# A hybrid attention layer on one core: where weight tiles are split into high and low halves, and when

## The chip, the cores and the metric

The kernel runs on one core of a Trainium2 chip. The metric is the device time of one launch in microseconds (us). The engines are TensorE (PE in the profile), VectorE (DVE), ScalarE (ACT), GpSimd (POOL) and SyncE (SP), whose queue starts most loads.

## The reference, cut to what matters

One layer, for 2048 tokens of width 1024 in float32. A normalised input is projected by one wide matrix; its columns feed three groups of heads, whose gated outputs are joined, multiplied by `w_out`, added to `x` and normalised again:

```python
def hybrid_layer(x, norm_g, w_in, ..., w_out):
    z = jnp.einsum('bsd,de->bse', rmsnorm(x, norm_g), w_in)
    (aq, ak, av, ag, mq, mk, mv, mo, mi, mf, mg, gq, gk, gv, ga, gg) = jnp.split(z, split_idx, axis=-1)
    y_a = band_chunk_attention(aq, ak, av, rel_bias) * jax.nn.silu(ag)      # 6 heads, band of 9 chunks of 64
    h_ml = mlstm_chunkwise(q, k, mv, mi, mf)                                # 6 heads, after a causal convolution
    y_b = jax.nn.sigmoid(mo) * head_rmsnorm(h_ml, ml_norm_g, 6) * jax.nn.silu(mg)
    y_c = head_rmsnorm(gla_chunkwise(gq, gk, gv, log_alpha), gla_norm_g, 4) * jax.nn.silu(gg)
    y = jnp.concatenate([y_a, y_b, y_c], axis=-1)
    return x + jnp.einsum('bse,ed->bsd', y, w_out)
# and at the end: rmsnorm(x, final_g)
```

In the gated linear attention (GLA) the part inside a chunk carries a decay for each pair of tokens and each key channel:

```python
    decay = jnp.where(causal, jnp.exp(jnp.minimum(bcum[:, :, None] - bcum[:, None, :], 0.0)), 0.0)
    att = jnp.einsum('bthd,bjhd,btjhd->bhtj', qx, kx, decay)
```

## The kernel before

**Split operands.** Every float32 operand of the large matmuls is held in two halves: a high half, which is a cast on ACT (line 231 for weights), and a low half, the tile minus its high half, by a subtraction (line 232). Three matmuls for each piece of the contraction take high by high, high by low and low by high (lines 240 to 242 and 260 to 262; 1199 to 1201 and 1209 to 1211 in the output projection). The function `other()` gives the engine of a subtraction: every third call gives GpSimd, the others VectorE. Weight tiles live in a ring of five (`wring`), and their raw loads in three buffers (`wraws`).

**First phase.** The tokens are taken in four blocks of 512. For each block the projections run on PE one weight tile after the other. Between pieces of a projection a small scheduler (`Flow`) lets "chains" advance: gates, mLSTM, GLA and the preparation of the next block. One chain is `gla_in`, the GLA diagonal. In each block, for two halves of 256 tokens, GpSimd does 16 steps of two multiplications: `gk` (line 790) is the key times the decay so far and `prd` (line 793) its product with the query. After every four steps PE reduces four `prd` tiles into the bank `pw` (line 799), and the next steps overwrite them. `flow.chains` holds the names of the chains that are active at that point of the program.

**Second phase.** Attention runs by blocks of tokens, too. For a head and 128 tokens PE makes scores (`s`, line 1068); DVE adds the bias and finds the maximum (`pt`, `sm`, line 1084), ACT takes the exponential (1087), DVE the reciprocal (1088) and POOL scales (`pt`, 1089). PE transposes `pt` into `tp` (1128); ACT casts it to `ph` (1134) and DVE subtracts to `pl` (1135), and PE multiplies both with the values (1144, 1147). After a head, `w` is copied to `cc` by ACT (1161) and DVE (1162); after two heads POOL multiplies with the gate `gt` (1164), and `cc` is split into the tile `y` (1105, 1106). The attention of the first block (`attention0`) runs beside the last kept projections, beside `load_wo`, and beside the first ten parts of the output projection `out_mm` for block 0. After that each block's attention is merged with `out_mm` of the block before it.

**load_wo.** The eight row tiles of `w_out` are loaded in the order k = 3 to 7, then 0, 1, 2. The first five go into the weight ring. The last three are split in halves of 512 columns into `xs` tiles, so that they appear as `x`: three loads, six casts (line 1035) and six subtractions (line 1036). `put` holds each split back by three and then calls `split_late`, which fixes its place in the program order. The output projection of block 0 uses k = 3 to 7 in its first parts, and these `x` tiles after them.

**Order.** PE's order is the order of the code. On the other engines a list scheduler places the instructions, except where `keep_in_program_order` or `issue_after` binds them. `merge(a, b, na, nb, acc)` alternates steps of two generators; a negative `acc` lets `a` go ahead first. `load_final` loads the two halves of `final_g`, after the attention's latest key load. The final addition of `x` is in `out_mm` (loads at line 1191, addition at 1214).

## Time and profile before

| what | value |
|---|---|
| median of three runs | 1271.97 us (1270.75 to 1275.88) |
| the profiled execution | 1273.61 us |
| its span, first to last instruction | 1271.7 us |
| mean granted TensorE clock | 0.989 |
| first phase, about | 0 to 925 us |

A page of the profile gives the busy time of each engine, then the span in 40 slices of 31.8 us with a digit for the busy tenths of each; PEclk is the granted clock of TensorE in tenths. A row of a timeline is: start, length, engine, line, operation, output <- inputs with sizes, count, and in brackets the idle time of the engine before it and what released it. A row of waits is: engine, tile and line of the waiting instruction, what it waited for; total us, times, longest. A row of windows gives for each engine the busy us and the number of instructions (x), then the granted clock, the DMA engines' share and GB/s.

### The profile page before, as it was taken

What the parts mean: (1) busy time and instruction counts of PE and PEld (TensorE: products, weight loads), DVE (VectorE), ACT (ScalarE), POOL (GpSimd) and SP (SyncE); (2) the same over time, 40 slices, a digit from 0 to 9 for tenths busy, and PEclk for the clock granted to TensorE, in tenths of its full rate; (3) what the DMA queues carried; (4) which work ended last, traced back from release to release, by engine and by line L of the source; (5) the groups of instructions that cost most, each with busy time, mean ns of one, the idle gap of its engine ahead of it and who ended that gap; (6) DMA issues with size and microseconds to landing.
All of it is one profiled execution on the core that took longest, in us unless ns stands there. A gap on an engine that the chain in (4) does not pass through costs nothing.

```text
span 1271.7 us, 19323 instructions
## 1 busy us (share of the span) xinstructions
PE 1243.1 (98%) x6804; PEld 1009.3 (79%) x6804; DVE 813.6 (64%) x1869; ACT 590.2 (46%) x1097; POOL 594.4 (47%) x762
## 2 busy tenths in 40 slices
PE   8999999999999999999999999999979999999997
PEld 7777877788787778878777877787867878878886
DVE  6647746772775677376487876664577676766641
ACT  5636422553543355253324643332566566655631
POOL 3337652244856233385523555641464454454442
PEclk8999999999999999999999999999989999999999
DMA  6158344434623443372353242427796456455122
GB/s 247 34 149 278 96 143 138 128 101 128 251 84 126 126 132 98 106 276 73 110 150 118 75 129 86 141 68 221 239 274 193 151 187 209 159 194 164 50 86 81
DMA packets 100185, 184.31 MB, mean 145 GB/s; under 512 B 10592, under 2 KB 46304, under 8 KB 100088
## 3 DMA queue, kind: packets, MB, share of 16 engines
q1 hardware_dynamic: 95624, 174.94, 43.8%
q10 hardware_dynamic: 4464, 8.13, 1.7%
q8 instruction: 54, 0.88, 0.3%
q14 instruction: 43, 0.35, 0.1%
HBM read 147.34 MB, written 35.70 MB: 144 GB/s over the span
## 4 chain that ended last, share of the span: by engine, by line
PE 89%; DVE 3%; POOL 3%; DMA 2%; issue 1%; ACT 1%; SPq 1%; POOLq 0%; DVEq 0%; ACTq 0%
PE ip L240 14%; PE ip L241 13%; PE ip L242 13%; PE ip L260 4%; PE ip L261 4%; PE ip L262 4%; PE ip L1209 4%; PE ip L1211 4%; PE ip L1210 4%; PE s L1068 4%; PE tp L1128 3%; PE ga L851 2%; PE w L1147 2%; PE s L705 2%; PE w L1144 2%
## 5 line engine op out<-in xcount | busy, mean ns | idle before, releaser
L240 PE MATMUL ip<-x,w 128*128 128x512 f32 x784 | 319.0, 407 | 0.2 <-ACT vg L519 0.2
L241 PE MATMUL ip<-x,w 128*128 128x512 f32 x784 | 306.8, 391 | 0.0
L242 PE MATMUL ip<-x,w 128*128 128x512 f32 x784 | 306.6, 391 | 0.0
L240 PEld LDWEIGHTS ip<-x,w 128*128 128x128 f32 x784 | 147.7, 188 | 43.7 <-issue 13.6
L242 PEld LDWEIGHTS ip<-x,w 128*128 128x128 f32 x784 | 147.7, 188 | 32.3
L241 PEld LDWEIGHTS ip<-x,w 128*128 128x128 f32 x784 | 147.8, 189 | 28.0 <-issue 1.4
L231 ACT CAST w<-wraw 128x1024 fp32r<-128x1024 f32 x126 | 131.7, 1047 | 37.2 <-PE ip L262 9.8
L232 POOL TENSOR_TENSOR w<-wraw,w 128x1024 fp32r<-128x1024 f32 x42 | 101.8, 2424 | 98.2 <-ACT w L231 98.2
L232 DVE TENSOR_TENSOR w<-wraw,w 128x1024 fp32r<-128x1024 f32 x84 | 114.7, 1367 | 41.7 <-ACT w L231 41.3
L1089 POOL TENSOR_SCALAR pt<-pt,sm 128x640 f32<-128x640 f32 (+2 forms) x96 | 72.5, 759 | 119.4 <-DVE sm L1088 91.7
L793 POOL TENSOR_TENSOR prd<-gk,zg 128x16 f32<-128x16 f32 (+7 forms) x112 | 65.7, 586 | 78.1 <-PE pw L799 72.2
L260 PE MATMUL ip<-w,x 128*128 128x512 f32 x256 | 102.0, 398 | 0.0
L261 PE MATMUL ip<-w,x 128*128 128x512 f32 x256 | 99.8, 390 | 0.2 <-POOL w L232 0.2
L262 PE MATMUL ip<-w,x 128*128 128x512 f32 x256 | 99.7, 390 | 0.0
L1087 ACT ACTIVATE pt<-pt,sm 128x640 f32<-128x640 f32 (+2 forms) x96 | 73.2, 763 | 47.4 <-DVE sm L1084 43.6
L1135 DVE TENSOR_TENSOR pl<-tp,ph 128x512 fp32r<-128x512 f32 (+1 forms) x108 | 71.9, 673 | 36.1 <-ACT ph L1134 35.9
L1068 PE MATMUL s<-kk,qq 128*128 128x256 f32 (+2 forms) x360 | 81.9, 313 | 2.3 <-DVE sm L1084 2.2
L790 POOL TENSOR_TENSOR gk<-gk,al 128x16 f32<-128x16 f32 (+14 forms) x120 | 70.7, 590 | 22.0 <-ACT al L767 14.6
L1134 ACT CAST ph<-tp 128x512 fp32r<-128x512 f32 (+1 forms) x108 | 60.3, 572 | 41.3 <-PE tp L1128 39.0
L490 ACT ACTIVATE e<-ip 128x512 f32<-128x512 f32 x44 | 26.2, 595 | 106.6 <-PE ip L242 102.5
L1068 PEld LDWEIGHTS s<-kk,qq 128*128 128x128 f32 x360 | 62.5, 189 | 16.3 <-DVE sm L1084 5.8
L1128 PE MATMUL tp<-ident,pt 128*128 128x128 f32 x420 | 62.5, 274 | 2.5 <-POOL pt L1089 2.5
(352 smaller groups left out, 2491.2 us busy)
## 6 DMA issues: line engine op xcount, KB each, us to landing
wraw<-in_w_f SPq DMA_DIRECT2D x100, 512.0 KB, 3.7
wraw<-in_w_t SPq DMA_DIRECT2D x28, 512.0 KB, 3.6
qq<-q_d SPq DMA_DIRECT2D x48, 256.0 KB, 4.6
kk<-k_d SPq DMA_DIRECT2D x18, 512.0 KB, 5.9
vv<-v_d SPq DMA_DIRECT2D x18, 512.0 KB, 6.2
xraw<-in_xT SPq DMA_DIRECT2D x16, 512.0 KB, 8.5
xr<-in_x SPq DMA_DIRECT2D x16, 512.0 KB, 3.7
out<-xr ACTq DMA_DIRECT2D x31, 256.0 KB, 2.3
```

The source lines that it names most:

```text
L231: nc.scalar.copy(w[:, :, 0, :], rv)
L232: other().tensor_tensor(w[:, :, 1, :], rv, f32(w[:, :, 0, :]), op=ALU.subtract)
L240: nc.tensor.matmul(ps, w[:, k, 0, :], X[k][:, 0, :], start=(k == 0), stop=False)
L241: nc.tensor.matmul(ps, w[:, k, 0, :], X[k][:, 1, :], start=False, stop=False)
L242: nc.tensor.matmul(ps, w[:, k, 1, :], X[k][:, 0, :], start=False, stop=(k == KT - 1))
L260: nc.tensor.matmul(ps, X[k][:, 0, t], w[:, 0, :], start=(k == 0), stop=False)
L261: nc.tensor.matmul(ps, X[k][:, 0, t], w[:, 1, :], start=False, stop=False)
L262: nc.tensor.matmul(ps, X[k][:, 1, t], w[:, 0, :], start=False, stop=(k == KT - 1))
L1068: nc.tensor.matmul(sp[:, :cn], qq[:, l, tt * P:(tt + 1) * P], kk[:, ko + c0:ko + c0 + cn], start=(l == 0), stop=(l == 1))
L1087: nc.scalar.activation(pt[:, :n], pt[:, :n], AF.Exp, bias=init, scale=-1.0, accum_out=sm[:, 2:3])
L1089: nc.gpsimd.tensor_scalar(pt[:, :n], pt[:, :n], sm[:, 3:4], 0.5, op0=ALU.mult, op1=ALU.mult)
L1128: nc.tensor.transpose(out=tp[:, w + x_ * P:w + (x_ + 1) * P], in_=pt[:, (b - b0) * P:(b - b0 + 1) * P], identity=ident)
```

## The change

Four edits. First, `other()` gives GpSimd no work while the chain `gla_in` is active: its count goes on, and the first call after the diagonal goes to GpSimd. Second, the six half tiles of the last three `w_out` rows are no longer split among the heads of the first block. They are kept in a list, and after the first attention and `load_wo` have been issued, they are split one after the other, behind the latest `ph` cast. Third, in the merge of block 1's attention with the rest of `out_mm(0)`, twice as many steps of attention go ahead. Fourth, `final_g` is loaded behind the latest load of values instead of keys.

```diff
     def other():
         turn["n"] += 1
-        return nc.gpsimd if turn["n"] % 3 == 0 else nc.vector
+        if turn["n"] < 3 or "gla_in" in flow.chains:
+            return nc.vector
+        turn["n"] = 0
+        return nc.gpsimd
...
+        rest = []
+
         def load_wo(Y):
...
                     for j in range(2):
                         w = wo[k, j] = xs.tile([P, 2, 512], FR, name="x")
-                        put(w, raw[:, 512 * j:512 * j + 512], other())
+                        rest.append((w, raw[:, 512 * j:512 * j + 512], other()))
...
-                with tc.issue_after(loads[-1]):
+                with tc.issue_after(vals[-1]):
                     nc.sync.dma_start(fg, final_g[512 * j:512 * j + 512].partition_broadcast(P))
...
-        loads = []
+        loads, vals = [], []
...
-            dma.dma_start(f32(vv[:, :nk // P, :]), v_d[h, :, kb // P:(kb + nk) // P, :])
+            vals.append(dma.dma_start(f32(vv[:, :nk // P, :]), v_d[h, :, kb // P:(kb + nk) // P, :]).ins)
...
-                nc.scalar.copy(ph[:, :w], tp[:, :w])
+                st["cast"] = nc.scalar.copy(ph[:, :w], tp[:, :w]).ins
...
         run_all(wl)
         for _ in range(left):
             next(parts)
+        with tc.issue_after(st["cast"]):
+            for e in rest:
+                split_late(*e)
...
-            run_all(merge(attention(q, YB, nxt), om, units * 10 + 8 * (units - 1), nb, -4 * nb if q == 1 else 0))
+            run_all(merge(attention(q, YB, nxt), om, units * 10 + 8 * (units - 1), nb, -8 * nb if q == 1 else 0))
```

Counted over the whole program, 21 of the 42 weight subtractions of line 232 on GpSimd go to VectorE, and two of the input tiles' subtractions (line 431) with them. The line numbers of the changed program are 3 to 5 higher in these functions.

How the order of the instructions changes, at three places. GpSimd in the third block, the last steps of the diagonal's first half (`gk` and `prd` of 14 to 16 times 16 columns; `tail` belongs to the convolution). Before:

```order
L556 COPY tail_4773<-u_4902 128x3
L790 TENSOR_TENSOR gk_4615<-gk_4615,al_4613 128x16x13
L232 TENSOR_TENSOR w_5182<-wraw_5183,w_5182 128x8x128
L793 TENSOR_TENSOR prd_183<-gk_4615,zg_4198 128x16x14
L555 COPY u_4996<-tail_2777 128x3
L790 TENSOR_TENSOR gk_4615<-gk_4615,al_4613 128x16x14
L555 COPY g_5099<-tail_2777 128x3
L793 TENSOR_TENSOR prd_183<-gk_4615,zg_4198 128x16x15
L556 COPY tail_4773<-g_4951 128x3
L790 TENSOR_TENSOR gk_4615<-gk_4615,al_4613 128x16x15
L793 TENSOR_TENSOR prd_183<-gk_4615,zg_4198 128x256
```

and now:

```order
L559 COPY tail_4773<-u_4902 128x3
L793 TENSOR_TENSOR gk_4615<-gk_4615,al_4613 128x16x13
L796 TENSOR_TENSOR prd_183<-gk_4615,zg_4198 128x16x14
L793 TENSOR_TENSOR gk_4615<-gk_4615,al_4613 128x16x14
L796 TENSOR_TENSOR prd_183<-gk_4615,zg_4198 128x16x15
L793 TENSOR_TENSOR gk_4615<-gk_4615,al_4613 128x16x15
L796 TENSOR_TENSOR prd_183<-gk_4615,zg_4198 128x256
L772 COPY gk_5029<-zg_4198 128x256
L558 COPY g_5099<-tail_2777 128x3
L558 COPY u_4996<-tail_2777 128x3
L559 COPY tail_4773<-g_4951 128x3
```

The weight's subtraction between step 14 and step 15 has gone, and three copies of convolution edges now come behind the last product.

ScalarE at the end of the first block's attention (`ph_8733` to `ph_8761` belong to its fifth head, `cc` and `y_7995` close a pair of heads). Before:

```order
L1161 COPY cc_8476<-w_8622 64x512
L1035 CAST x_8549<-xr_8547 128x512
L1035 CAST x_8552<-xr_8547 128x512
L1035 CAST x_8559<-wraw_8557 128x512
L1035 CAST x_8562<-wraw_8557 128x512
L1134 CAST ph_8733<-tp_8728 128x512
L1134 CAST ph_8742<-tp_8737 128x512
L1035 CAST x_8571<-xr_8569 128x512
L1035 CAST x_8574<-xr_8569 128x512
L1134 CAST ph_8761<-tp_8758 128x256
L1087 ACTIVATE pt_8751,sm_8752<-pt_8751,sm_8752 128x640
L1105 CAST y_7995<-cc_8476 128x512
```

and now, further on, at the first head of block 1 (`ph_8892` is that head's first cast, `y_7996` the last tile `y` of block 0):

```order
L1092 ACTIVATE pt_8833,sm_8834<-pt_8833,sm_8834 128x640
L1139 CAST ph_8892<-tp_8887 128x512
L1092 ACTIVATE pt_8876,sm_8877<-pt_8876,sm_8877 128x640
L1110 CAST y_7996<-cc_8712 128x512
L1040 CAST x_8549<-xr_8547 128x512
L1040 CAST x_8550<-xr_8547 128x512
L1040 CAST x_8555<-wraw_8553 128x512
L1040 CAST x_8556<-wraw_8553 128x512
L1040 CAST x_8563<-xr_8561 128x512
L1040 CAST x_8564<-xr_8561 128x512
L1139 CAST ph_8905<-tp_8900 128x512
L1139 CAST ph_8914<-tp_8909 128x512
```

The six `x` casts stood ahead of three `ph` casts of block 0, and now stand between the first and the second `ph` cast of block 1.

VectorE at the same two places. Before, with `x` subtractions ahead of `pl_8734` and `pl_8762`:

```order
L1162 TENSOR_TENSOR cc_8476<-w_8622,cc_8476 64x512
L1036 TENSOR_TENSOR x_8552<-xr_8547,x_8552 128x512
L1036 TENSOR_TENSOR x_8559<-wraw_8557,x_8559 128x512
L1084 ISA pt_8751,sm_8752<-s_8718,bt_67,sm_8752 128x256
L1084 ISA sm_8752 128x1
L1135 TENSOR_TENSOR pl_8734<-tp_8728,ph_8733 128x512
L1084 ISA pt_8783,sm_8784<-s_8768,mz_7982 128x384
L1084 ISA sm_8784 128x1
L1135 TENSOR_TENSOR pl_8743<-tp_8737,ph_8742 128x512
L1036 TENSOR_TENSOR x_8571<-xr_8569,x_8571 128x512
L1036 TENSOR_TENSOR x_8574<-xr_8569,x_8574 128x512
L1135 TENSOR_TENSOR pl_8762<-tp_8758,ph_8761 128x256
```

and now, ahead of `pl_8906`, the second of block 1's first head:

```order
L1140 TENSOR_TENSOR pl_8893<-tp_8887,ph_8892 128x512
L1093 RECIPROCAL sm_8877<-sm_8877 128x1
L1041 TENSOR_TENSOR x_8550<-xr_8547,x_8550 128x512
L1089 ISA pt_8920,sm_8921<-s_8897,bt_67,sm_8921 128x256
L1089 ISA sm_8921 128x1
L1041 TENSOR_TENSOR x_8555<-wraw_8553,x_8555 128x512
L1089 ISA pt_8952,sm_8953<-s_8931,mz_7982 128x384
L1089 ISA sm_8953 128x1
L1041 TENSOR_TENSOR x_8563<-xr_8561,x_8563 128x512
L1041 TENSOR_TENSOR x_8564<-xr_8561,x_8564 128x512
L1140 TENSOR_TENSOR pl_8906<-tp_8900,ph_8905 128x512
L1140 TENSOR_TENSOR pl_8915<-tp_8909,ph_8914 128x512
```

Four subtractions have moved behind the first block's attention; the other two of the six have moved on GpSimd in the same way, behind the subtraction of `y_7996`.

## The prediction

> **What bounds the kernel now.** I read the page first: the busy times, then the slices.

> ```profile
> PE 1243.1 (98%) x6804; PEld 1009.3 (79%) x6804; DVE 813.6 (64%) x1869; ACT 590.2 (46%) x1097; POOL 594.4 (47%) x762
> PE   8999999999999999999999999999979999999997
> PEclk8999999999999999999999999999989999999999
> ```

> TensorE (PE) is busy 98% of a span of 1271.7 us. Its matmuls are the same before and after, so the change can give only what PE loses: 1271.7 - 1243.1 = 28.6 us of idle, and some clock. Both show in slice 31 (922 to 954 us): 7 tenths busy, clock 8. That is where the projections have run out and the last output-weight tiles are split beside attention. Next, the list of PE's waits, by line and releaser (total us, times, longest):

> ```profile
> PE w L1144 <- ACT ph L1134: 5.0, 3, 3.8
> PE w L1147 <- DVE pl L1135: 3.7, 7, 1.9
> PE tp L1128 <- POOL pt L1089: 2.5, 2, 1.9
> PE pw L799 <- POOL prd L793: 1.8, 1, 1.8
> PE ip L261 <- POOL w L232: 0.2, 1, 0.2
> ```

> Four long waits of 3.8, 1.9, 1.9 and 1.8 us carry it. Only one of the eight diagonals' product groups ever stops PE (pw L799, once), and a weight's low half hardly ever does (0.2 us). Now the windows around slice 31 (window, length, busy us of PE, PEld, DVE, ACT, POOL with counts, then clock, DMA share and GB/s), and PE's timeline in it:

> ```profile
> 930.00:940.00 10.00, 9.13 (x55) 7.26 (x54) 9.14 (x27) 7.69 (x18) 9.49 (x10) 1.00 1.04 266
> 940.00:950.00 10.00, 5.26 (x29) 3.99 (x27) 4.53 (x7) 4.93 (x10) 4.39 (x4) 0.85 1.04 292
> 950.00:960.00 10.00, 7.90 (x40) 6.19 (x40) 9.15 (x25) 5.99 (x15) 4.43 (x5) 0.81 0.70 240
> 960.00:970.00 10.00, 8.08 (x41) 6.58 (x40) 5.84 (x18) 5.50 (x12) 4.31 (x5) 0.83 0.81 255
> ```
> ```profile
> 929.70 0.50 PE L1144 MATMUL w<-ph,vv 128*128 128x384 f32 x2 [0.89 <-ACT ph L1134]
> ...
> 943.96 0.51 PE L1068 MATMUL s<-kk,qq 128*128 128x384 f32 x2
> 948.32 0.79 PE L1144 MATMUL w<-ph,vv 128*128 128x512 f32 x1 [3.85 <-ACT ph L1134]
> 950.99 0.69 PE L1147 MATMUL w<-pl,vv 128*64 128x512 f32 x1 [1.88 <-DVE pl L1135]
> 951.47 0.63 PE L1199 MATMUL ip<-w,hl 128*128 128x512 f32 x1
> 951.90 0.63 PE L1200 MATMUL ip<-w,hl 128*128 128x512 f32 x1
> ...
> 954.69 0.33 PE L1147 MATMUL w<-pl,vv 128*64 128x256 f32 x1 [0.42 <-DVE pl L1135]
> ...
> 963.88 0.36 PE L1128 MATMUL tp<-ident,pt 128*128 128x128 f32 x1 [1.92 <-POOL pt L1089]
> ```

> Two things are to be seen. After 944.47 PE stands still for 3.85 us, does one matmul, and waits 1.88 us more. And the clock falls behind each long wait: a matmul is issued every 0.43 us at 951.47, and the windows grant 0.85, 0.81 and 0.83, while the 0.89 us wait at 929.70 left its window at 1.00. So a wait here has a second price. The timelines of ACT and DVE say why PE waited:

> ```profile
> 945.61 1.14 ACT L1035 CAST x<-xr 128x512 fp32r<-128x512 f32 x2 [4.14 <-DMA xr<-in_w_o]
> 946.65 1.13 ACT L1035 CAST x<-wraw 128x512 fp32r<-128x512 f32 x2
> 947.69 1.06 ACT L1134 CAST ph<-tp 128x512 fp32r<-128x512 f32 x2
> ```
> ```profile
> 946.77 1.35 DVE L1036 TENSOR_TENSOR x<-xr,x 128x512 fp32r<-128x512 f32 x1 [4.56 <-ACT x L1035]
> 948.04 1.76 DVE L1036 TENSOR_TENSOR x<-wraw,x 128x512 fp32r<-128x512 f32 x1
> ...
> 950.25 0.69 DVE L1135 TENSOR_TENSOR pl<-tp,ph 128x512 fp32r<-128x512 f32 x1
> ...
> 951.92 2.38 DVE L1036 TENSOR_TENSOR x<-xr,x 128x512 fp32r<-128x512 f32 x2
> 954.22 0.41 DVE L1135 TENSOR_TENSOR pl<-tp,ph 128x256 fp32r<-128x256 f32 x1
> ```

> ACT sat 4.14 us at the head of its queue for a w_o tile that was still coming from HBM. The ph cast that PE needed was queued behind that cast. DVE then did its x subtractions (1.35 and 1.76 us) before the pl that PE needed.

> **The subtractions off GpSimd.** The other stall lies in the diagonal at 565 us: POOL's timeline, and PE's clock behind it.

> ```profile
> 558.18 2.84 POOL L232 TENSOR_TENSOR w<-wraw,w 128x1024 fp32r<-128x1024 f32 x1
> ...
> 564.98 1.13 POOL L790 TENSOR_TENSOR gk<-gk,al 128x240 f32<-128x240 f32 x1
> 566.19 0.97 POOL L793 TENSOR_TENSOR prd<-gk,zg 128x256 f32<-128x256 f32 x1
> ```
> ```profile
> 568.00:569.00 1.00, 1.00 (x4) 0.76 (x4) 0.98 (x1) 1.00 (x3) 0.96 (x1) 0.55 0.07 29
> 569.00:570.00 1.00, 1.00 (x4) 0.81 (x3) 1.00 (x3) 0.40 (x1) 1.00 (x3) 0.50 0.00 0
> 570.00:571.00 1.00, 1.00 (x4) 0.79 (x3) 0.96 (x2) 0.00 (x0) 0.92 (x2) 0.50 0.81 193
> 571.00:572.00 1.00, 1.00 (x5) 0.73 (x4) 0.96 (x2) 0.00 (x0) 0.92 (x2) 0.75 0.74 299
> ```

> The last product group ends at 567.16 and PE had waited 1.8 us for it. POOL did a weight's subtraction of 2.84 us in the middle of it. Without it, and with the tail copies that the new order puts behind the group, POOL ends by 564.3 at the latest, about 1 us before PE asks (567.2 - 1.8 = 565.4). The wait goes, and with it the slow clock: 0.45 + 0.50 + 0.50 + 0.25 = 1.7 us of work lost. **1.8 + 1.7 = 3.5 us.**

> [...]

> The subtractions go to DVE. The groups by line (busy us and mean ns of one, then idle before them and its releaser):

> ```profile
> L232 POOL TENSOR_TENSOR w<-wraw,w 128x1024 fp32r<-128x1024 f32 x42 | 101.8, 2424 | 98.2 <-ACT w L231 98.2
> L232 DVE TENSOR_TENSOR w<-wraw,w 128x1024 fp32r<-128x1024 f32 x84 | 114.7, 1367 | 41.7 <-ACT w L231 41.3
> ```

> The order has 21 fewer of them on POOL and 21 more on DVE: 21 x 1.367 = 28.7 us, so DVE goes from 64% to about 66%. What hides them is the weight ring of five tiles: PE waited 0.2 us in all for any low half, though POOL's copies take 2.42 us. DVE is idle ahead of its own for 41.7 us in total, waiting for ACT's cast: mostly it is free when a tile comes. I cost this at 0; what it costs if that fails is the rival on the slow side. The input tiles' subtractions (two more on DVE) have no wait row at all: 0. The other seven diagonals made PE wait nowhere, so freeing them gains 0.

> The moved work still meets the diagonal, since DVE and POOL slow each other. Two of POOL's steps, one alone and one behind a weight's subtraction on DVE:

> ```profile
> 533.64 0.43 POOL L793 TENSOR_TENSOR prd<-gk,zg 128x128 f32<-128x128 f32 x1
> ...
> 544.70 1.46 POOL L793 TENSOR_TENSOR prd<-gk,zg 128x144 f32<-128x144 f32 x1
> ```
> ```profile
> 543.73 2.10 DVE L232 TENSOR_TENSOR w<-wraw,w 128x1024 fp32r<-128x1024 f32 x1 [3.83 <-ACT w L231]
> ```

> A step can so lose about 1.0 us to one subtraction. One of them in the last steps fits into the 1.1 us of room above (564.3 to 565.4); two would leave a wait of 0.9 us, too short to slow the clock, going by 929.70: the term would be 2.6. I take 3.5: before, one weight tile was split in these steps, and the tiles keep their order. [...]

> **The late tiles' split behind the first attention.** ACT's six x casts, four of the six subtractions on DVE and two on POOL move past the last two heads' mixing of tokens 0 to 511. PE's own order is the same up to the transpose at 963.88, so its two waits in front go: 3.85 + 1.88 = 5.7 us. So does the 0.42 us at 954.69, whose pl stood behind the 2.38 us of x subtractions. The windows from 940 to 960 lost 1.5 + 1.9 = 3.4 us of clock, about half of it while PE stood still anyway; I take 1.6 us lost to work, near the 1.7 of the diagonal's stall. The wait at 963.88 stays: its chain (PE, ACT's cc, DVE's cc, POOL's gate multiply, then pt) starts from PE and shifts with it. **5.7 + 0.4 + 1.6 = 7.7 us.**

> Now the price. The casts, 6 x 0.57 = 3.4 us, and DVE's four subtractions, 2.38/2 = 1.2 us at best and 1.35 at worst here, 4.8 to 5.4 us, stand ahead of the next ph/pl pairs of the first new head (pl_8906, pl_8915). Counted from PE's restart at the pt wait: PE first has three pairs of scores (0.4 to 0.5 us each), eight transposes, one ph/pl pair and two projection parts of 3 x 0.43 us at the slow clock, by my estimate 5.4 us, and then asks for pl_8906. DVE can start after ACT's first two casts, 1.0 us behind the restart, and then has four subtractions (5 us), two score reductions between them (0.5 us each) and pl (0.7): 7.6 us. So PE waits about 7.6 - 5.4 = 2.2 us and loses 1.6 us of clock, as behind each wait of 1.8 us or more above: **3.8 us given back**. From below: if DVE starts the subtractions while PE still waits for pt, it is 0 to 1 us and no clock. From above: two such waits, one at each of pl_8906 and pl_8915: 7.6 us.

> The 9 attention steps instead of 5 ahead of the first remaining part only take filler away: two parts of 3 x 0.21 us (half of 0.43, the clock being full) no longer stand before the first ph/pl of that head. The cover that is left is the scores and transposes; if it fails, 1.3 us. The same parts run later, so their work is not lost. I take 0.

> The loads. final_g (two of 256 KB) goes behind the next q and v loads, so the two w_o loads land earlier; nothing in front waits for them any more, and the multiply with final_g comes after a whole output tile. The x tile of the first output rows is loaded behind a gate tile and is wanted about 10 us later, with the queue at a DMA share of 0.81 to 1.04: 0, at worst another wait as above, 3.8.

> **The sum.** 3.5 + 7.7 - 3.8 = 7.4 us. The profiled execution took 1273.6 us in all (span 1271.7): it becomes 1266.2. The median of the three runs, 1271.97, lies 1.6 below it: 1264.6. I forecast **1264.5**.

> **The rivals.** *All the stalls go* (0.25): DVE and ACT find room in PE's remaining wait, nothing is given back: 3.5 + 7.7 = 11.2, so 1260.8; were the pt wait at 963.88 to go as well (1.9 + 1.6), 1257.3. For it: DVE busy only 5.84 of 10 us in 960 to 970. Against it: four subtractions of 1.2 us in one piece ahead of pl_8906.

> *The stall only moves* (0.17): two new waits on pl, or one on x's low half or its load too, cost 7.6 and undo the split's gain; only the diagonal's 3.5 stays: 1268.5.

> *The change does not do what it says* (0.05): two moved subtractions hold up the last steps of the diagonal at 565 us, and the products still come late. For it: the 1.46 us beside 0.43. Against it: a step lost 1.0 there, not more. With the whole stall back, 7.7 - 3.8 = 3.9 stays: 1268.

> *Slower* (0.08): DVE becomes the late one in the diagonals. Place: a weight's low half, now behind convolution work on DVE, when the ring of five has run down. Price: each such wait of 1.8 us costs 3.5 with its clock. There are eight diagonals; two waits eat the gain, and from four on it is slower by over 0.5%: 4 x 3.5 - 7.4 = +6.6, 1278.6; with one in each, +20.6. For it: DVE was 0.96 to 1.00 busy in the windows at 568 to 572. Against: the 0.2 us wait, and 41.7 us of idle before DVE's own subtractions. [...]

> **How the numbers follow.** About 0.5% (6.4 us) is what a measurement of this kernel can tell from no change: faster means under 1265.6, slower over 1278.3. The forecast case has 0.45; it spans about 1262 to 1267 (the give-back at 1 to 6 us), and some two thirds of it lie under 1265.6: 0.30. With the 0.25 of no new stall that is 0.55 faster. The rest of the forecast case (0.15), the moved stall (0.17) and the unchanged diagonal (0.05) are 0.37 within 0.5%. Slower: 0.08. The range takes in all stalls gone (1257.3) and the forecast with both of its unknown costs at their upper ends (1264.6 + 3.8 + 1.3 = 1269.7), each with 1.2 us more, by which the lowest run lies under the median: 1256.1 to 1270.9.

> **What would show it.** Right: no wait on prd at L799 and clock 1.00 at 560 to 572; no wait of over 1 us on ph or pl ahead of the pt wait; no w_o load as releaser of an ACT cast with ph behind it; behind the pt wait, one wait of about 2 us on pl with x subtractions in front of it on DVE. Wrong: waits of ip on DVE's w (L232) in the diagonals, which would make it slower; two or more long waits behind 956 us, which would make it the moved stall; or a pl that comes in time, which would make it 1261.

## The result, and the profile after

The changed kernel takes 1264.24 us (median of 8 runs, 1263.53 to 1271.32), the kernel before beside it 1271.96 us. The ratio is 0.9948 (95% interval 0.9932 to 0.9964): 6.6 us faster. The forecast was 1264.5 us. The profiled execution took 1265.87 us with a span of 1264.2, that is 7.5 us less span than before. The total came out almost exactly, but by luck: several of its terms were off and cancelled, as the trace shows.

The page of the changed kernel, busy times and two rows of slices:

```profile
PE 1241.0 (98%) x6804; PEld 1008.3 (80%) x6804; DVE 808.9 (64%) x1892; ACT 588.7 (47%) x1097; POOL 552.7 (44%) x739
PE   9999999999999999999999999999998999999997
PEclk7999999999999999999999999999999999999999
```

PE's idle time is 1264.2 - 1241.0 = 23.2 us, 5.4 less than before. The 7 of the slice from 922 to 954 us is gone (counted from one it is the thirtieth, which the prediction called 31); an 8 stands in the slice behind it, 948 to 980 us, and the clock has its 9 in both. DVE took over 21 weight subtractions and is nevertheless busy for 5 us less. The waits of PE, total, times, longest:

```profile
PE s L1073 <- DVE sm L1089: 3.2, 5, 0.9
PE tp L1133 <- POOL pt L1094: 2.5, 2, 1.9
PE w L1152 <- DVE pl L1140: 2.3, 5, 1.1
PE ip L1215 <- POOL x L1041: 1.6, 1, 1.6
...
PE w L1149 <- ACT ph L1139: 0.9, 1, 0.9
```

The 3.8 us on ph, the 1.9 us on pl and the 1.8 us on prd are gone; the 1.9 us on pt is there as before. New are 1.6 us on the first x tile and 1.1 us on a pl, in this order (PE's timeline):

```profile
946.07 0.50 PE L1149 MATMUL w<-ph,vv 128*128 128x512 f32 x1
...
952.82 0.77 PE L1133 MATMUL tp<-ident,pt 128*128 128x128 f32 x5 [1.90 <-POOL pt L1094]
...
956.53 0.50 PE L1215 MATMUL ip<-x,y 128*128 128x512 f32 x1 [1.61 <-POOL x L1041]
...
959.99 0.45 PE L1152 MATMUL w<-pl,vv 128*64 128x256 f32 x2 [1.13 <-DVE pl L1140]
```

The windows of the same stretch and of the diagonal show what the prediction did not have: a clock that stays up (window, length, busy us of each engine, clock, DMA share, GB/s).

```profile
560.00:570.00 10.00, 10.00 (x51) 7.68 (x50) 7.51 (x10) 6.03 (x10) 6.32 (x13) 1.00 0.17 57
940.00:950.00 10.00, 9.31 (x59) 7.49 (x57) 8.02 (x27) 6.72 (x15) 4.61 (x5) 1.00 0.97 292
950.00:960.00 10.00, 5.36 (x35) 4.20 (x33) 8.63 (x18) 7.82 (x17) 7.46 (x6) 1.00 0.93 295
960.00:970.00 10.00, 10.00 (x58) 8.57 (x59) 8.20 (x23) 6.29 (x15) 5.52 (x6) 1.00 0.73 230
```

From 950 to 960 us PE is idle for 4.6 us, in three waits of 1.90, 1.61 and 1.13 us, and the clock stays at 1.00. Before, the same wait on pt (1.92 us) was followed by half clock.

Since PE's order is fixed, one matmul can be found in both traces, and the difference of its start times is a ledger. The third edit changes PE's order between the wait on pt and the start of block 2 (963.88 to 1040 us before), so no row stands there; at each row PE has the same work behind it in both traces.

| up to this matmul of PE | before, us | after, us | difference | step |
|---|---|---|---|---|
| first phase, after the start | 208.25 | 209.28 | +1.03 | +1.0: slow clock at the start lasts longer (-1.4 to +2.2 in the other profiles) |
| projection ahead of the diagonal's products | 559.28 | 560.32 | +1.04 | 0 |
| projection behind them | 573.12 | 570.19 | -2.93 | -4.0 |
| attention of block 0 | 937.30 | 934.64 | -2.66 | +0.3 |
| `ph` times values, last head pair of block 0 | 957.12 | 946.07 | -11.05 | -8.4 |
| first scores of block 2 | 1041.78 | 1031.52 | -10.26 | +0.8 |
| projection, block 2's attention begun | 1049.36 | 1041.85 | -7.51 | +2.7 |
| projection near the end | 1258.45 | 1250.90 | -7.55 | 0 |

The +0.8 is about the two new waits above (2.7 us) less the 1.7 us of clock that the kernel before lost behind its wait on pt. The step of +2.7 us near 1035 us was in no forecast. There PE meets two short waits and then a slow clock (timeline and windows of the changed kernel):

```profile
1034.22 1.14 PE L1073 MATMUL s<-kk,qq 128*128 128x384 f32 x4 [0.56 <-DVE sm L1089]
...
1036.86 1.43 PE L1073 MATMUL s<-kk,qq 128*128 128x384 f32 x4 [0.81 <-DVE sm L1089]
```
```profile
1036.00:1038.00 2.00, 1.19 (x5) 0.86 (x5) 1.57 (x8) 0.72 (x3) 2.00 (x4) 0.76 0.07 25
1038.00:1040.00 2.00, 2.00 (x7) 1.71 (x6) 1.40 (x6) 1.66 (x4) 1.16 (x2) 0.50 0.10 36
```

### The profile page after: what moved, and what is told of

The parts are those of the page before. It is cut to its first block, busy times and chain, and to the rows that moved or that the text cites. A ratio compares the mean times of both kernels' runs of the same rounds, so it can differ in the third digit from the quotient of the medians.

```text
span 1264.2 us, 19306 instructions
## 1 busy us (share of the span) xinstructions
PE 1241.0 (98%) x6804; PEld 1008.3 (80%) x6804; DVE 808.9 (64%) x1892; ACT 588.7 (47%) x1097; POOL 552.7 (44%) x739
## 4 chain that ended last, share of the span: by engine, by line
PE 92%; DVE 3%; issue 2%; POOL 2%; ACT 1%; DMA 1%; POOLq 0%; DVEq 0%; ACTq 0%
PE ip L243 15%; PE ip L244 14%; PE ip L245 14%; PE ip L263 4%; PE ip L265 4%; PE ip L264 4%; PE ip L1214 4%; PE ip L1216 4%; PE ip L1215 4%; PE s L1073 4%; PE tp L1133 3%; PE w L1152 2%; PE ga L854 2%; PE w L1149 2%; PE s L708 2%
## 5 line engine op out<-in xcount | busy, mean ns | idle before, releaser
L235 DVE TENSOR_TENSOR w<-wraw,w 128x1024 fp32r<-128x1024 f32 x105 | 134.9, 1284 | 65.3 <-ACT w L234 64.3
L1094 POOL TENSOR_SCALAR pt<-pt,sm 128x640 f32<-128x640 f32 (+2 forms) x96 | 71.8, 751 | 114.7 <-DVE sm L1093 96.6
L796 POOL TENSOR_TENSOR prd<-gk,zg 128x16 f32<-128x16 f32 (+7 forms) x112 | 69.6, 622 | 106.5 <-PE pw L802 100.5
L793 POOL TENSOR_TENSOR gk<-gk,al 128x16 f32<-128x16 f32 (+14 forms) x120 | 75.6, 630 | 22.3 <-ACT al L770 14.6
L235 POOL TENSOR_TENSOR w<-wraw,w 128x1024 fp32r<-128x1024 f32 x21 | 50.2, 2389 | 61.4 <-ACT w L234 61.4
L1223 POOL TENSOR_TENSOR xr<-xr,e 128x512 f32<-128x512 f32 x31 | 40.5, 1307 | 55.5 <-ACT jk L1221 52.2
```

What stands on the lines that cost most here:

```text
L235: other().tensor_tensor(w[:, :, 1, :], rv, f32(w[:, :, 0, :]), op=ALU.subtract)
L793: nc.gpsimd.tensor_tensor(b16(gk)[:, :, 0:c], b16(gk)[:, :, 0:c], b16(al)[:, :, c:c + 1].broadcast_to([P, NB, c]), op=ALU.mult)
```

## The experiments

All ratios are to the kernel before, run beside each kernel on the same chip, with their 95% intervals; there are 6 or 12 runs of each kernel and 11 to 23 of the one before. "Run" with a number names an experiment below.

**1 and 2: the two main edits alone.** Run one takes only the new `other()`:

```diff
-        return nc.gpsimd if turn["n"] % 3 == 0 else nc.vector
+        if turn["n"] < 3 or "gla_in" in flow.chains:
+            return nc.vector
+        turn["n"] = 0
+        return nc.gpsimd
```

> Only the first edit on the kernel before: no weight subtraction on GpSimd during a diagonal. Theory of the prediction: the wait on prd at 565 us goes and nothing takes its place, 3.5 to 4 us faster than before (about 1268), with the stall at 944 us as before. Rival: the time of the diagonal was only lent, and the moved subtractions make VectorE late for weights: within 1 us of before or slower, with waits of ip on VectorE's w.

1269.4 us, ratio 0.9979 (0.9966 to 0.9992): 2.7 us faster, between 1.0 and 4.3. No wait on prd and none of ip on a low half remains, and the stall at 944 us is there, with 3.3 us of waits on ph and 3.9 on pl (the longest on ph is 1.8 us here, where it was 3.8). The theory holds; its size is a little small, though the interval takes in 3.5. In this profile's ledger the diagonal brings the same 4.0 us as above (-1.24 at 559 us, -5.21 at 573 us), against the one profile of before.

Run two has only the late split (with `rest`, `st["cast"]`; `acc` stays `-4 * nb`, `final_g` behind the keys).

> Only the second edit on the kernel before: the six half tiles are split behind the first attention; merge start and loads of final_g as before. If the merge start matters, TensorE asks for the first x tile right behind the wait on pt, and waits about 3 us more for its low half: 8 us gained in front, 5 or more given back, about 1269. If it does not matter: 8 gained, about 3 given back, as in the changed kernel, about 1267.

1269.63 us, ratio 0.9973 (0.996 to 0.9985): 3.4 us faster. The two edits add up within their intervals: 2.7 + 3.4 = 6.1 of the 6.6 us. The time is that of the first case expected (about 1269); what the start of the merge has to do with it is seen in run three. In this profile's ledger 8.4 us are gained in front, 4.4 given back before block 2 and nothing at its start. Also, this run has the diagonal's stall unchanged, and it shows its price anew:

```profile
569.36 0.62 PE L799 MATMUL pw<-prd,hs 128*32 128x256 f32 x2 [1.76 <-POOL prd L793]
```
```profile
570.00:571.00 1.00, 1.00 (x5) 0.82 (x6) 0.83 (x1) 1.00 (x4) 0.92 (x2) 1.00 0.01 4
571.00:572.00 1.00, 1.00 (x6) 0.83 (x5) 1.00 (x3) 0.55 (x1) 1.00 (x2) 1.00 0.00 0
```

It is the same wait, 1.76 us behind the same product, and here the clock stays at 1.00. So whether the 1.7 us of clock that the prediction laid on this wait are lost is a matter of the execution.

**3 and 4: the two small edits undone.** Run three is the changed kernel with `-4 * nb`:

```diff
-            ... nb, -8 * nb if q == 1 else 0))
+            ... nb, -4 * nb if q == 1 else 0))
```

> The changed kernel with the third edit undone (half as many attention steps ahead of the rest of the projection of block 0). Theory A: the third edit hides the late splits, so without it the first x tile is awaited 2 to 4 us longer and the kernel is 2 to 4 us slower than the changed one (1266 to 1268). Theory B: the third edit causes the loss of 3.2 us near 1035 us, where the parts it left over meet the start of the next block; without it that loss goes, and the kernel is about as fast as the changed one or up to 3 us faster (1261 to 1264).

1266.19 us, ratio 0.9955 (0.9938 to 0.9972), against 0.9948 for the changed kernel: no difference that can be told. The trace says why. PE asks for the first x tile earlier and waits longer, and then finds pl ready:

```profile
951.29 0.33 PE L1133 MATMUL tp<-ident,pt 128*128 128x128 f32 x1 [1.91 <-POOL pt L1094]
954.97 0.79 PE L1215 MATMUL ip<-x,y 128*128 128x512 f32 x1 [2.79 <-POOL x L1041]
```

2.79 us in one wait instead of 1.61 + 1.13 = 2.74 in two, and the clock falls here (6.8 us at 0.50, against none at this place in the changed kernel). Theory A's mechanism is right (2.8 instead of 1.6 on x), but it left out that pl gives it back. Theory B is right about the place: the loss near 1035 us is tied to the third edit. In the ledgers of runs one to three, which have `-4 * nb` like the kernel before, the start of block 2 (1041.78 to 1049.36 us before) takes the same time as before to 0.01 us. In the eight profiles with `-8 * nb` (the changed kernel's two and runs four, five, eight and ten to twelve) it takes 1.5 to 3.5 us more, and 1.5 to 2.3 even in the five of them in which the clock stays up there. ScalarE's rows show the chain, before and in the changed kernel:

```profile
1038.16 0.62 ACT L1105 CAST y<-wraw 128x512 fp32r<-128x512 f32 x1 [2.43 <-DMA wraw<-y_d]
```
```profile
1030.30 0.62 ACT L1110 CAST y<-wraw 128x512 fp32r<-128x512 f32 x1 [3.12 <-DMA wraw<-y_d]
```

ScalarE stands at the head of its queue for the load of a late tile `y` of block 1; behind this cast come the copies to `cc`, the last tile's split (`hl`) and the addition of the residual, and only then VectorE's first score reduction of block 2. In the four profiles with `-4 * nb` the cast starts 3.6 us before PE's first scores of block 2, and the reduction follows 0.8 us behind them. With `-8 * nb` it starts 0.5 to 1.6 us before them, the reduction comes 1.7 to 2.8 us behind, and PE waits on sm. So the third edit wins time at the x tile (up to block 2, run three's ledger gives back 4.5 us, much of it clock, the changed kernel's 0.8) and loses time at block 2; in these medians the two cancel.

Run four moves the loads of `final_g` back behind the keys (`issue_after(loads[-1])`).

> The changed kernel with the fourth edit undone (final_g behind the keys). Theory of the prediction: the place of these loads costs nothing, within 1 us of the changed kernel (1263 to 1265). Rival: the two loads stand ahead of the output weights again, ScalarE's x casts come later, and the wait on the first x tile grows by 1 to 3 us (1265 to 1267).

1266.16 us, ratio 0.9948 (0.993 to 0.9966), the changed kernel's own. The wait on x is 1.6 us again. The fourth edit costs and brings nothing that can be told here.

**5 and 10: which engine gets the first output tile.** The six late subtractions are dealt anew:

```diff
-                        rest.append((w, raw[:, 512 * j:512 * j + 512], other()))
+                        rest.append((w, raw[:, 512 * j:512 * j + 512], nc.vector if j == 0 else nc.gpsimd))
```

> The changed kernel, with the engines of the six late subtractions dealt anew: the three halves that the first output tile needs go to VectorE, the other three to GpSimd. Theory: the wait of 1.6 us on the first x tile comes from its place on GpSimd behind two pt and the low half of y, and the wait of 1.1 us on pl from four subtractions ahead of it on VectorE; so the first falls to under 0.7 and the second to under 0.6 us, 1.5 us faster than the changed kernel in the trace. Rival: GpSimd, with three of them, delays the next pt, and a wait of transposes on pt of 1 us or more takes their place.

The place of the first x tile on GpSimd in the changed kernel was this, behind two pt and the low half of `y`:

```profile
951.97 1.57 POOL L1094 TENSOR_SCALAR pt<-pt,sm 128x640 f32<-128x640 f32 x2
953.51 1.30 POOL L1111 TENSOR_TENSOR y<-cc,y 128x512 fp32r<-128x512 f32 x1
954.76 1.71 POOL L1041 TENSOR_TENSOR x<-xr,x 128x512 fp32r<-128x512 f32 x1
```

With the new deal there is no wait on x at all, and the waits on pt are as before; the rival is out. The wait on pl stays at 1.1 us, although one subtraction less stands before it: PE comes for it earlier by the wait that it no longer has. 1264.24 us, ratio 0.9931 (0.9908 to 0.9954). I ran it again beside the changed kernel:

> The changed kernel once more, beside the next three on one chip, for a direct comparison: 7 to 8 us under before (ratio 0.993 to 0.996). Of the price of a wait: if the slow clock follows each wait of 1.8 us, the clock dips again behind the wait on pt; if it depends on the run, this profile shows dips elsewhere than the first one, with the same waits.

> The kernel whose first output tile's halves are subtracted on VectorE, again: if its gain is real, 1.5 us under the changed kernel beside it (in idle time), about 1262 where that one has 1264. If only the clock differed, the two medians agree within 1 us.

The changed kernel has 1265.47 us here (ratio 0.9939, 0.9918 to 0.9959), this one 1263.27 us (0.9922, 0.9897 to 0.9947). The gain of about 2 us appears both times, and is what the trace promises, but the intervals overlap. The profiles hold a lesson on the clock. Here is the second profile of the new deal, behind its wait on pt (PE's timeline, then windows):

```profile
951.46 0.77 PE L1133 MATMUL tp<-ident,pt 128*128 128x128 f32 x5 [1.91 <-POOL pt L1094]
```
```profile
952.00:954.00 2.00, 2.00 (x12) 1.90 (x10) 2.00 (x4) 2.00 (x5) 2.00 (x3) 0.64 1.03 313
954.00:956.00 2.00, 2.00 (x8) 1.60 (x8) 2.00 (x4) 2.00 (x5) 2.00 (x2) 0.51 1.03 385
```

In this execution the clock did fall behind the wait on pt, and the wait on pl is not there: PE, at half clock, came later than DVE. In the first profile of the same program the clock stayed up there, PE waited for pl, and the clock fell near 1035 us instead. In the changed kernel's second profile it fell neither there nor at 1035, but at 1128 us.

**6 and 7: more attention steps first, and the splits spread.** Run six is the changed kernel with `-16 * nb`.

> The changed kernel with the rest of the projection of block 0 started after twice as many attention steps again (16 instead of 8 in the merge's start). Theory: the wait on the first x tile (1.6 us) goes altogether, but the wait on pl (1.1 us), which stands behind the same subtractions, stays or grows to 2 or 3 us, since less projection work stands before it; net within 2 us of the changed kernel. Rival: both go, 2.7 us faster.

1270.59 us, ratio 0.9975 (0.9961 to 0.9989): by the ratios some 3.5 us slower than the changed kernel, more than the theory allowed. Part of it is the start of block 2, where PE waits 3.0 us on sm at once: ScalarE's cast there starts only 2.4 us after the first scores, behind 4.3 us of waiting for its load. The wait on x goes, and the wait on pl takes its place, with DVE's subtractions ahead of it as in the theory, but grown to 3.6 us (PE's timeline, then DVE's):

```profile
958.57 0.69 PE L1152 MATMUL w<-pl,vv 128*64 128x256 f32 x2 [3.57 <-DVE pl L1140]
```
```profile
953.87 1.35 DVE L1041 TENSOR_TENSOR x<-wraw,x 128x512 fp32r<-128x512 f32 x1
...
955.62 1.89 DVE L1041 TENSOR_TENSOR x<-xr,x 128x512 fp32r<-128x512 f32 x2
957.43 0.47 DVE L1089 CUSTOM_DVE_ANT_0 pt<-s,bt,sm 128x256 f32<-128x256 f32 x1
957.83 1.28 DVE L1140 TENSOR_TENSOR pl<-tp,ph 128x512 fp32r<-128x512 f32 x2
```

Run seven keeps that start and issues one split at every second step:

```diff
-        with tc.issue_after(st["cast"]):
-            for e in rest:
-                split_late(*e)
...
-            run_all(merge(..., -8 * nb if q == 1 else 0))
+            for i, _ in enumerate(merge(..., -16 * nb if q == 1 else 0)):
+                if rest and i % 2:
+                    split_late(*rest.pop(0))
```

> The changed kernel, the six late splits issued one at every second step of block 1's attention instead of in one piece, and the projection's rest started after 16 as in the run with that number. Theory: no pl stands behind more than one subtraction and no x tile is awaited, so the 1.6 and 1.1 us waits go: 1 to 3 us faster than the changed kernel in idle time. Rival: the steps of attention without projection work between them cannot cover the chain from transpose to pl, so that waits of 0.5 to 1 us on ph and pl appear at each of them and eat the gain.

1266.02 us, ratio 0.9941 (0.9923 to 0.9958). The 3.6 us wait is gone, in place of it come 0.35 and 1.35 us on pl: 1.7 us instead of the changed kernel's 2.7. So the piece of four subtractions was the cause, and spreading it helps; the shortened cover takes a good part back, as the rival said. At the start of block 2 there is a wait of 1.8 us on sm; ScalarE's cast starts 1.2 us behind the first scores there. The time agrees with the changed kernel's within the intervals.

**8: VectorE's reserve.** All weight subtractions go to VectorE until the attention is set up: 124 of the 126, and a few of the input tiles' with them.

```diff
-        if turn["n"] < 3 or "gla_in" in flow.chains:
-            return nc.vector
-        turn["n"] = 0
-        return nc.gpsimd
+        return nc.gpsimd if "rest" in turn and turn["n"] % 3 == 0 else nc.vector
...
         rest = []
+        turn["rest"] = 0
```

> The changed kernel with the remaining weight subtractions of the first phase taken off GpSimd as well, so that VectorE does all 126. It measures VectorE's reserve, on which the prediction's rival on the slow side rests. Theory: the ring of five tiles still hides them, no wait of ip on VectorE's w above 0.5 us, within 1 us of the changed kernel. Rival: VectorE is near its limit, and waits of ip on w appear in every block, 3 us slower or more.

1266.21 us, ratio 0.995 (0.9932 to 0.9968): the changed kernel's own. No wait of ip on a VectorE low half appears anywhere. VectorE is not near its limit in the first phase: it still sits idle for 67.3 us in all ahead of these 124 subtractions, 66.3 of them for ScalarE's casts. But the profiled execution of this run (span 1271.6) has a wait of 5.9 us of another kind, on PE and on DVE:

```profile
970.95 0.69 PE L1150 MATMUL w<-pl,vv 128*64 128x384 f32 x2 [5.93 <-DVE pl L1138]
```
```profile
969.07 0.69 DVE L1217 TENSOR_TENSOR xr<-ip,xr 128x512 f32<-128x512 f32 x1 [7.67 <-DMA xr<-in_x]
...
970.23 0.67 DVE L1138 TENSOR_TENSOR pl<-tp,ph 128x512 fp32r<-128x512 f32 x1
```

DVE stood at the head of its queue for the residual's x tile, with pl behind it. That load takes its buffer over from a raw `w_out` tile, and since the split is late, the buffer is late: in the changed kernel the load was issued at 956.50 us, right after GpSimd's subtraction of that tile (954.76 + 1.71 = 956.47), and the addition follows at 961.51. In the kernel before it was issued at 948.20 and added at 969.07, so that it had some 20 us to land. What is left of this room depends on the landing, 4.0 us in the changed kernel's first profile, 7.0 in its second and 11.0 in run eight (issued at 957.60); why it differs, no run shows. The changed kernel's second profile shows it too, milder: 3.26 us on DVE and 2.1 us on PE.

```profile
962.94 0.69 DVE L1219 TENSOR_TENSOR xr<-ip,xr 128x512 f32<-128x512 f32 x1 [3.26 <-DMA xr<-in_x]
```

**11 and 12: the residual's tile early.** The last three raw tiles are staged so that the first x tile finds a buffer that is already free:

```diff
             for n, k in enumerate((3, 4, 5, 6, 7, 0, 1, 2)):
+                if n == 5:
+                    turns[0] += 1
+                if n == 7:
+                    split_late(*lag.pop(0))
                 raw = stage()
```

> The changed kernel, with the raw tiles of the last three output weight rows staged so that the first x tile of the residual finds a free buffer and is loaded before block 1's attention instead of after the late splits. Theory: in the changed kernel that load waits for the late subtraction to free its buffer (issued at 956.5, added at 961.5 us), and in some executions it lands too late and stops TensorE for up to 6 us; so the median is at most 1 us lower here, but no run lies 5 us above the fastest. Rival: the load is never late enough, or the earlier split and loads delay the output weights: no change, or 1 to 2 us slower.

> Both together: the halves of the first output tile on VectorE, and the residual's first tile loaded early. Theory: the waits on the first x tile (1.6 us) and on a late residual tile are both gone, 1 to 3 us under the changed kernel, about 1261 to 1263, with a smaller spread. Rival: as for each of the two.

The load is issued at 932.85 us and no DVE row waits for it. 1264.11 us, ratio 0.9932 (0.9912 to 0.9952), six runs within 1263.1 to 1265.9, against 1265.47 for the changed kernel beside it. Together with the new deal 1263.36 us, ratio 0.9923 (0.9902 to 0.9943). This last kernel beats the one before by 9.8 us (0.77% of 1272.26); its lead over the changed kernel (2.1 us by the medians) is of the size of the removed waits, but the intervals overlap, so the timing alone does not show it. Nor do six runs prove that the late runs of the changed kernel (1269.8 and 1271.3 us) came from this load; their mean clocks were also low (0.991 and 0.990).

## Why the prediction was right, and where it was not

**The diagonal.** Right in mechanism. GpSimd's last product ends at 562.5 us, and PE begins its reduction at 565.9:

```profile
561.84 0.65 POOL L796 TENSOR_TENSOR prd<-gk,zg 128x256 f32<-128x256 f32 x1
...
566.55 0.50 POOL L796 TENSOR_TENSOR prd<-gk,zg 128x16 f32<-128x16 f32 x1 [3.22 <-PE pw L802]
```

The room is at least 3.4 us, where I had reckoned with 1.1. The term was 3.5; alone on the chip the edit brings 2.7 (1.0 to 4.3). The idle part, 1.8, is there in both profiles that have the wait. The clock part, 1.7, depends on the execution.

**VectorE's extra work at 0.** Right, and its reserve is larger than thought (run eight). The mean subtraction even became shorter, on both engines:

```profile
L235 DVE TENSOR_TENSOR w<-wraw,w 128x1024 fp32r<-128x1024 f32 x105 | 134.9, 1284 | 65.3 <-ACT w L234 64.3
L235 POOL TENSOR_TENSOR w<-wraw,w 128x1024 fp32r<-128x1024 f32 x21 | 50.2, 2389 | 61.4 <-ACT w L234 61.4
```

One on DVE takes 1.284 us in the mean instead of 1.367, and one on GpSimd 2.389 instead of 2.424. In both traces a subtraction on DVE takes 1.21 to 1.23 us where GpSimd is idle beside it; those with GpSimd busy for more than half of their time average 1.52 us before and 1.36 in the changed kernel. The rival that moved subtractions would hold up the diagonal did not come true: the steps between 546 and 562 us take 0.5 to 1.6 us, three subtractions of 1.23 to 1.35 us beside them, and still end early. Only one of the three falls among the last four products, though, as I had assumed, so two of them there were not tried.

**The late split, front.** 7.7 forecast, 8.4 in the ledger of this pair of profiles: the two waits and the small one are gone, and so is their slow clock.

**The late split, given back.** The term was 3.8 us: 2.2 idle at pl and 1.6 of clock. Idle, it is 1.61 + 1.13 = 2.7 us. The larger part is the first x tile's low half on GpSimd, which I had named only in a rival; the pl wait is half of what I gave it. (I took a subtraction at 1.35 us at worst, although the row at 948.04 us shows 1.76; in the new place they take 1.64, 1.35 and 0.95 twice, and their sum of 4.9 us is as forecast.) The clock part did not come in this profile, and the slow clock behind the wait on pt, which I had left in place, went too: the ledger has +0.8 where I had +3.8. Near 1035 us it has +2.7, 1.7 of them clock behind two waits of under 1 us, where I had nothing. In the ledger the gains are 4.0 + 8.4 against 3.5 + 7.7, and the losses 0.8 + 2.7 at the two places and 1.0 at the start against 3.8: too much was taken back at 956 us, too little elsewhere, and the total was right because these errors cancel.

**The step that failed** is the price of a wait: "So PE waits about 7.6 - 5.4 = 2.2 us and loses 1.6 us of clock, as behind each wait of 1.8 us or more above". One profile showed two waits of 1.8 to 1.9 us with a slow clock behind them (on prd and on pt), and I made a rule of it. Over the profiles the wait on pt is 1.9 us everywhere: the clock falls to 0.50 right behind it in before, run one, run seven, run eight and run ten, and stays at 1.00 in the changed kernel's two profiles and in runs four, five, eleven and twelve (runs two, three and six have a longer wait close behind it). Nor does it take one long wait: in the changed kernel the clock fell to 0.50 at 1037 us behind waits of 0.56 and 0.81 us, 2.6 us apart.

```profile
960.63:964.04 3.41, 1.49 (x13) 1.17 (x11) 2.73 (x10) 2.75 (x6) 2.27 (x3) 1.00 0.77 197
```
```profile
948.30:951.72 3.42, 2.62 (x18) 1.96 (x16) 2.81 (x11) 2.50 (x5) 1.80 (x2) 1.00 0.72 232
951.72:955.13 3.41, 2.11 (x14) 1.69 (x14) 2.07 (x3) 3.41 (x8) 3.41 (x5) 1.00 0.94 280
```

Over all profiles, from 25 to 1250 us, a window at full clock with PE busy for less than 45% of it was followed by half clock in 12 of 12 cases, one of 45 to 62% in 9 of 25, and one above that never; near the start (5 to 11 us) it fell behind windows of 69 to 87%, so busy time alone does not decide. In these profiles, then, the half clock goes with the idle time that one window collects, and where the edges fall differs between executions: counted from the first instruction, they lie 1.2 us apart in the changed kernel's two profiles (slow stretches begin at 1037.04 and 1128.00 us).

**The third and fourth edits at 0.** The times agree with 0 (runs three and four). For the third the reason was wrong: "The same parts run later, so their work is not lost" leaves out where they run. It gains at the x tile and loses 1.5 us or more at the start of block 2, and the 0 is the difference.

**The residual's load.** I gave it 0, at worst 3.8, and the cause as a gate tile ahead of it in the queue. Its issue waits for the buffer, its landing took 4 to 11 us, and the worst wait seen is 5.9 us on PE.

## What to carry to other kernels

An instruction that waits for a load at the head of its engine's queue stops all that is queued behind it (ScalarE for 4.14 us in the kernel before, VectorE for 7.67 us in run eight); move it behind the urgent work, but then look at which buffers it frees, since the loads that take them over move as well. When a block of side work is moved, deal it by who needs its result first, and keep it in pieces shorter than the cover at the new place. Cost a TensorE wait at its idle time, and add the clock as a chance rather than as a fixed price: half clock came right behind the same wait of 1.9 us in 5 of the 11 profiles that have no longer wait close behind it. Short waits close together can cost it as one long wait does (0.56 and 0.81 us, 2.6 us apart, in the changed kernel). When two traces are compared by the start of one matmul, take points that have the same work behind them.

## What was not expected of the hardware

The runs of one and the same kernel spread over 9 us, and most of it goes with TensorE's mean granted clock. In 56 runs of the kernel before, spans go from 1267.4 to 1277.0 us and clocks from 0.993 to 0.987; the ten runs at 0.993 have a mean span of 1268.2, the two at 0.987 of 1275.6. A line through the 56 falls by about 1.1 us for each 0.001 (correlation -0.80). The changed kernel's 14 runs average 0.9936 against 0.9906: by that slope some 3 us of its gain is clock that shorter and fewer waits leave it, an estimate. One profile shows one draw: a change of 2 us in such a kernel is seen in its idle time sooner than in its median.
